# The first four blocks of the input projection computed together, chunk by chunk, with six blocks held in PSUM until the row scale is there

## The chip, the cores and the metric

The kernel runs on one NeuronCore of one Trainium2 chip. The metric is device microseconds of one launch. Engines are named as in the profile: PE is the matmul engine (TensorE), DVE is VectorE, ACT is ScalarE, POOL is GpSimd, and SP issues the transfers. Each engine works through its own instructions in a fixed order; semaphores make one engine wait for another.

## The reference

Two transformer-like blocks stand one behind the other, on one sequence of 512 rows of 1024 features, in float32. The change sits in the input projection of the first block. Cut to that, the reference is:

```python
def rms_norm(x, g):
    y = x * lax.rsqrt(jnp.mean(x * x, axis=-1, keepdims=True) + 1e-5)
    return y * g

def first_block(x, ...):                      # x: 1 x 512 x 1024
    xn = rms_norm(x, mix_norm)
    proj = xn @ w_in + b_in                   # 1024 -> 4352
    q, k, v, cb, cc, cx, ga, gc = split(proj) # 512, 128, 128, 3 x 512, 2 x 1024
    attn = sliding_window_attention(q, k, v, sinks)   # 8 heads, 2 KV heads, window 128
    conv = cb * causal_depthwise_conv(cc * cx, conv_w)
    merged = sigmoid(ga) * (attn @ w_attn_branch) + sigmoid(gc) * (conv @ w_conv_branch)
    h = x + merged @ w_out
    up = causal_depthwise_conv(rms_norm(h, ffn_norm) @ w_up, ffn_conv_w)
    gate, val = split(up)
    h = h + (silu(gate) * val) @ w_down       # 2816 hidden
    return rms_norm(h, final_norm)
```

The second block projects again, mixes with a sparse attention, a stick-breaking attention and a gated recurrence, projects out and ends in a layer norm. The change does not touch it.

## The kernel before

**Layout and products.** Activations lie transposed: a tile is 128 features by 512 rows of the sequence, and the model's 1024 features are eight such chunks (`KT = 8`). A weight block is 128 output features by all 1024 inputs (512 KB). To keep float32 accuracy each operand is split into a high and a low part: ACT writes the high part (`A.copy`, or `A.activation` with the norm's weight as scale), DVE subtracts it from the original for the low part (`split_w` for weights, `split` for x). One chunk of one block is then three PE products of 128x512: high weights by high x, high weights by low x, low weights by high x. A block is 24 products into one PSUM bank; the input projection has 34 blocks.

**The row scale.** The projection is done on x times the norm's weight, not yet divided by each row's root mean square. That row scale (`rstd1`, a 128x512 tile) comes from squares that ACT and DVE add up into one tile, one matmul with ones (`rms_scale`, bank `gb`) and a chain: a `tensor_scalar` on DVE, Ln and Exp on ACT, and four DVE steps (one Newton step). Each finished block is multiplied by it as it leaves its bank (`scaled`), and only then is the bank free. Before, blocks 0 and 1 are computed, the row sum's matmul is called for behind block 1 (`pre` at `n == 1`), and the block loop goes on.

**Banks and buffers.** The eight banks are pools: `m` 2, `ga` 2, `gb` 2, `oa` 1, `ob` 1. Blocks 0 to 3 take `m`, `oa`, `m`, `ob` (`alt`), later ones take `m`. Attention uses `ga` and `gb` for scores and transposes and `oa`, `ob` for its output. Raw weights (`raw`), high parts (`wh`) and low parts (`wl`) have two buffers each.

**The order of the work.** All weights and x come through SP's queue, in the program's order. `drive` interleaves the projection and the attention as generators, by the costs that they yield: attention advances at a quarter of the projection's rate, once blocks 0 to 5 (four of queries, one of keys, one of values) are done. A scheduler then fixes each engine's order. At the start block 0's weights come in three pieces between the chunks of x, and ten small matmuls on a tile of ones (`WARM`) occupy PE until the first data are there.

The rest of the kernel has the same pattern: weight blocks streamed through two buffers, products on PE, and elementwise work between.

Of the kernel before, what the change touches and what calls it, by code (L numbers as in the profile page):

```python
# [18 lines left out]
P = 128  # L19
T = 512  # L20
D = 1024
KT = 8
# [31 lines left out]
        IN2[(_n, _i) if _c else _n] = len(IN2)  # L54


WARM = 10
RATE_A = [0.593, 0.587, 0.591, 0.741, 0.778]
RATE_B = [0.318, 0.367, 0.286, 0.332, 0.497]
ORDER = [('gf', 0), ('gq', 0), 'kc', ('gi', 0), 'ng', 'vc', ('nq', 0), ('gf', 1), ('gq', 1), ('nq', 2), 'kw', 'ks', 'vs', ('bq', 0), ('gi', 1), ('gf', 2), 'vw', ('bk', 0), ('nq', 1), ('bv', 0), ('gq', 2), ('gi', 2), ('bq', 1), ('bk', 1), ('bv', 1)]  # L60
# [6 lines left out]
def tile_net(ctx, tc, a, out):  # L67
    nc = tc.nc
# [112 lines left out]
    def raw_tile():  # L181
        return wp.tile([P, 8, P], F32, tag="raw", name=nm("raw"), bufs=2)
# [6 lines left out]
    def split_w(raw, cuts=(0, 8)):  # L189
        nk, w = raw.shape[1], raw.shape[2]  # L190
        wh = wp.tile([P, 8, P], F32R, tag="wh", name=nm("wh"), bufs=2)[:, :nk, :w]
        wl = wp.tile([P, 8, P], F32R, tag="wl", name=nm("wl"), bufs=2)[:, :nk, :w]
        with tc.high_priority(offset=100):
            for c0, c1 in zip(cuts, cuts[1:]):
                c = slice(c0, min(c1, nk))
                A.copy(wh[:, c], raw[:, c])  # L196
                tt(wl[:, c], raw[:, c], wh[:, c].bitcast(F32), ALU.subtract)
        return wh, wl
# [45 lines left out]
    def alt(n):  # L244
        return ("m", "oa", "m", "ob")[n % 4]

    def split(src, scale=None, new=None):
        h, l = new(F32R), new(F32R)
        if scale is None:
            A.copy(h, src)  # L250
            tt(l, src, h.bitcast(F32), ALU.subtract)
        else:
            A.activation(h, src, AF.Copy, scale=scale)
            stt(l, src, scale, h.bitcast(F32), ALU.mult, ALU.subtract)
        return h, l
# [19 lines left out]
    def rms_scale(sq, dst):  # L275

        ps = bank("gb")
        for n, s in enumerate(sq):
            mm(ps, ones, s, n == 0, n == len(sq) - 1)
        ms = wk()  # L280
        V.tensor_scalar(ms, ps, 1.0 / D, 1e-5, ALU.mult, ALU.add)
        rsqrt(ms, dst)
# [14 lines left out]
        return cp.tile([P, T], F32, tag="rs", name=n, bufs=1)  # L297


    smt = cp.tile([P, SMW], F32, tag="smt", name="smt")  # L300
    nc.sync.dma_start(smt, a["small"])
    W1 = Weights([(a["w_in"][n], 8) for n in range(34)])
    raw = raw_tile()
    W1.raw.append(raw)
    xin = []
    cuts = (0, 2, 4, 8)
    for k in range(KT):
        t = tl("np")
        nc.sync.dma_start(t, a["xT"][k])
        xin.append(t)  # L310
        if k < 3:
            c = slice(cuts[k], cuts[k + 1])
            nc.sync.dma_start(raw[:, c], a["w_in"][0, :, c])
        elif k == 5:
            W1.ahead(2, 0)
    W1.ahead(3, 0)
    cst = cp.tile([P, CMW], F32, tag="cst", name="cst")
    nc.sync.dma_start(cst, a["const"])

    def S(n, i=0, w=None):  # L320
        o, full = SM[n]
        return smt[:, o + i:o + i + (full if w is None else w)]
# [19 lines left out]
        mm(warm[:, 0:P], ones, ones)  # L342


    W1.w.append(split_w(raw, cuts))
    xs = [split(xin[k], S("mix", k, 1), xt) for k in range(KT)]
    sq = []
    with tc.issue_after(last_act()):
        for k in range(KT):
# [12 lines left out]
    rstd1 = rs_tile("rs1")  # L362
# [86 lines left out]
        return use  # L449

    def in_proj():
        hold = []
        for n in range(34):
            yield from dense(W1, xs, use_in(n), (lambda: rms_scale(sq[:1], rstd1)) if n == 1 else None,
                             alt(n) if n < 4 else "m", hold=hold if n < 2 else None)

    def softmax_a(j, ip):

# [151 lines left out]
    for i in range(2):  # L610
        oh = wk()
        nc.sync.dma_start(oh[0:33], a["onehot"][:, 512 * i:512 * i + 512])
        ps = bank("ga")
# [635 lines left out]
    for half in range(2):  # L1249
        ps = [bank(t) for t in (("ga", "ga", "oa", "ob"), ("m", "m", "gb", "gb"))[half]]  # L1250
# [96 lines left out]
def _blocks(w):  # L1347
    k, n = w.shape
    return w.reshape(k // P, P, n // P, P).transpose(2, 1, 0, 3)


def _layout(i):
    pair = lambda step: np.concatenate([np.r_[64 * j:64 * j + 64, 64 * (j + step):64 * (j + step) + 64] for j in range(step)])
    q1 = pair(4)
    cin = [q1, 512 + np.arange(256)]
    for j in range(4):
        for base in (1280, 1792, 768):
            cin.append(base + P * j + np.arange(P))
    for j in range(8):
        for base in (2304, 3328):  # L1360
            cin.append(base + P * j + np.arange(P))
    cin = np.concatenate(cin)
    q2 = pair(3)
    off = np.cumsum([0, 384, 128, 128, 128, 128, 128, 128, 18, 384, 256, 256, 256, 256, 384, 384, 384, 384])
    nq, kc, vc, ks, vs, kw, vw, ng, nz, bq, bk, bv, bz, gq, gf, gi, gz = off[:-1]
    r = np.arange
    cin2 = np.concatenate([
        nq + q2, kc + r(128), vc + r(128), ks + r(128), vs + r(128), kw + r(128), vw + r(128),
        bq + r(256), bk + r(256), bv + r(256), gq + r(384), gf + r(384), gi + r(384),
        nz + q2, bz + r(256), gz + r(384),  # L1370
    ])
    rmix = np.concatenate([q2, r(384, 1024)])
    f = np.float32
    w_in, w_in2 = i["w_in"][0], i["w_in_2"][0]
    const, cmi, oh = _constants()
    pos = i["cmp_pos_2"][0].reshape(16, 2, 64).transpose(2, 1, 0).reshape(64, 32)
    small = {
        "mix": _cols(i["mix_norm"][0]), "ffn": _cols(i["ffn_norm"][0]), "fin": _cols(i["final_norm"]),
        "bin": _cols(i["b_in"][0][cin]),
        "cw": i["conv_w"][0].reshape(3, 4, P).transpose(2, 1, 0).reshape(P, 12),  # L1380
        "fcw": i["ffn_conv_w"][0].reshape(3, 44, P).transpose(2, 1, 0).reshape(P, 132),
        "sink": np.broadcast_to(i["sinks"][0], (P, 8)),
        "pos": np.concatenate([pos, pos], axis=0),
        "hgn": _cols(i["hg_norm_w_2"][0]), "lb": _cols(i["hg_lb_2"][0]),
    }
    up = _blocks(i["w_up"][0])
    br = np.concatenate([_blocks(i["w_attn_branch"][0][q1]), _blocks(i["w_conv_branch"][0])], axis=2)
    wo2 = i["w_out_2"][0][rmix]
    return {
        "xT": i["x"][0].T.reshape(KT, P, T),  # L1390
        "small": np.concatenate([small[n] for n in SM], axis=1),
        "const": const, "cmask": cmi, "onehot": oh,
        "tbl": np.concatenate([i["rel_bias_2"], np.full((1, 6), NEG, f)], axis=0),
        "w_in": _blocks(w_in[:, cin]),
        "w_br": br,
        "w_out": _blocks(i["w_out"][0]),
        "w_up": np.stack([up[:NFF], up[NFF:]], axis=1).reshape(2 * NFF, P, KT, P),
        "w_down": _blocks(i["w_down"][0]),
        "w_in_2": _blocks(w_in2[:, cin2]),
        "w_gate": w_in2[:, ng:ng + 18].reshape(KT, P, 18).transpose(1, 0, 2),  # L1400
        "w_ck1": i["w_ck1_2"][0].reshape(16, P, P).transpose(1, 0, 2), "w_ck2": i["w_ck2_2"][0],
        "w_cv1": i["w_cv1_2"][0].reshape(16, P, P).transpose(1, 0, 2), "w_cv2": i["w_cv2_2"][0],
        "w_out_2": wo2.reshape(KT, P, 2, T).transpose(2, 0, 1, 3),
        "ln_g": i["ln_g_2"], "ln_b": i["ln_b_2"],
    }
# [17 lines left out]
```

## Time and profile before

| | |
|---|---|
| median of 3 runs | 1068.86 us (1068.28 to 1069.32) |
| the profiled execution | 1068.53 us |
| its span, first to last instruction | 1066.8 us |
| PE busy | 1039.5 us, 97% of the span |
| DVE, ACT, POOL busy | 704.4 us (66%), 488.8 us (46%), 44.0 us (4%) |
| DMA | 97.84 MB, mean 92 GB/s |
| mean granted TensorE clock | 0.999 of 2.4 GHz |

The span is the time from the first to the last instruction of the profiled execution; 1.7 us of its own time lie around it. Busy shares are averages over the whole kernel. A matmul's duration in the trace includes the pipeline's tail, so two that follow each other overlap; the pace is read from start to start.

### The profile page before, as it was taken

What the parts mean: (1) busy time and instruction counts of PE and PEld (TensorE: products, weight loads), DVE (VectorE), ACT (ScalarE), POOL (GpSimd) and SP (SyncE); (2) the same over time, 40 slices, a digit from 0 to 9 for tenths busy, and PEclk for the clock granted to TensorE, in tenths of its full rate; (3) what the DMA queues carried; (4) which work ended last, traced back from release to release, by engine and by line L of the source; (5) the groups of instructions that cost most, each with busy time, mean ns of one, the idle gap of its engine ahead of it and who ended that gap; (6) DMA issues with size and microseconds to landing.
All of it is one profiled execution on the core that took longest, in us unless ns stands there. A gap on an engine that the chain in (4) does not pass through costs nothing.

```text
span 1066.8 us, 14636 instructions
## 1 busy us (share of the span) xinstructions
PE 1039.5 (97%) x5712; PEld 838.9 (79%) x5712; DVE 704.4 (66%) x1313; ACT 488.8 (46%) x855; POOL 44.0 (4%) x89
## 2 busy tenths in 40 slices
PE   8999999999999999999999999999999999989997
PEld 6788888888888888888877888767777777767886
DVE  6876643356448777777763233597967698887757
ACT  5754443322344444444442222433625676578740
POOL 0000000000220000000000111200000000011000
PEclk9999999999999999999999999999999999999999
DMA  6212232333432233223335333531321110101232
GB/s 218 79 60 80 79 94 85 99 99 109 142 120 85 98 99 99 98 99 99 99 94 193 97 106 90 184 101 41 99 75 47 59 41 22 41 21 37 82 120 79
DMA packets 32801, 97.84 MB, mean 92 GB/s; under 512 B 4878, under 2 KB 5390, under 8 KB 32732
## 3 DMA queue, kind: packets, MB, share of 16 engines
q1 hardware_dynamic: 32732, 96.91, 28.7%
q8 instruction: 45, 0.74, 0.3%
q14 instruction: 24, 0.20, 0.1%
HBM read 94.77 MB, written 5.27 MB: 94 GB/s over the span
## 4 chain that ended last, share of the span: by engine, by line
PE 75%; DVE 11%; ACT 7%; DMA 3%; issue 2%; SPq 1%; POOL 1%; DVEq 0%; POOLq 0%; ACTq 0%
PE pm L139 44%; PE pob L139 12%; PE poa L139 12%; PE pga L139 4%; PE pgb L139 3%; DVE wl L136 2%; DMA raw<-in_w_in 1%; ACT wh L196 1%; DVE lv L136 1%; DMA raw<-in_w_down 1%; DVE hk L136 1%; DVE dk L136 1%; DVE np L136 1%; DVE nk L942 1%; ACT nk L948 1%
## 5 line engine op out<-in xcount | busy, mean ns | idle before, releaser
L139 PE MATMUL pm<-x,wh 128*128 128x512 f32 (+1 forms) x1360 | 433.4, 395 | 2.1 <-DVE x L133 0.9
L139 PEld LDWEIGHTS pm<-x,wh 128*128 128x128 f32 (+1 forms) x1360 | 252.2, 187 | 58.5 <-issue 3.5
L196 ACT CAST wh<-raw 128x1024 fp32r<-128x1024 f32 (+1 forms) x153 | 156.7, 1025 | 275.8 <-issue 109.9
L139 PE MATMUL pm<-x,wl 128*128 128x512 f32 (+1 forms) x680 | 268.3, 395 | 0.0
L136 DVE TENSOR_TENSOR wl<-raw,wh 128x1024 fp32r<-128x1024 f32 (+1 forms) x153 | 181.9, 1189 | 89.5 <-ACT wh L196 87.7
L139 PEld LDWEIGHTS pm<-x,wl 128*128 128x128 f32 (+1 forms) x680 | 127.0, 187 | 26.8 <-issue 1.6
L139 PE MATMUL poa<-x,wh 128*128 128x512 f32 x208 | 65.0, 394 | 0.0
L139 PE MATMUL pob<-x,wh 128*128 128x512 f32 x208 | 64.1, 390 | 0.0
L139 PE MATMUL pm<-np,wh 128*128 128x512 f32 x176 | 54.1, 389 | 0.0
L136 DVE TENSOR_TENSOR dk<-pm,rs 128x512 f32<-128x512 f32 x43 | 29.5, 686 | 28.1 <-PE pm L139 28.0
L139 PEld LDWEIGHTS poa<-x,wh 128*128 128x128 f32 x208 | 39.0, 188 | 9.3 <-issue 1.0
L139 PEld LDWEIGHTS pob<-x,wh 128*128 128x128 f32 x208 | 39.0, 188 | 8.0
L136 DVE TENSOR_TENSOR nk<-pm,rs 128x512 f32<-128x512 f32 x34 | 23.4, 687 | 32.6 <-PE pm L139 32.4
L139 PE MATMUL poa<-x,wl 128*128 128x512 f32 x104 | 40.6, 390 | 0.1
L139 PE MATMUL pob<-x,wl 128*128 128x512 f32 x104 | 40.6, 390 | 0.0
L139 PEld LDWEIGHTS pm<-np,wh 128*128 128x128 f32 x176 | 33.0, 188 | 6.8
L139 PE MATMUL pm<-np,wl 128*128 128x512 f32 x88 | 34.2, 389 | 0.0
L948 ACT ACTIVATE nk<-nk,q 128x128 f32<-128x128 f32 (+3 forms) x48 | 26.5, 555 | 11.5 <-DVE q L946 11.2
L942 DVE CUSTOM_DVE_ANT_0 nk<-pgb,bi 128x128 f32<-128x128 f32 (+3 forms) x48 | 23.1, 484 | 7.9 <-PE pgb L139 7.2
L133 DVE SCALAR_TENSOR_TENSOR dk<-nk,smt,dk 128x511 f32<-128x511 f32 (+1 forms) x34 | 25.4, 748 | 1.4 <-ACT dk L435 0.8
L139 PE MATMUL pgb<-np,np 128*128 128x128 f32 (+3 forms) x96 | 25.9, 351 | 0.4 <-DVE nk L967 0.3
L133 DVE SCALAR_TENSOR_TENSOR nk<-nk,smt,nk 128x511 f32<-128x511 f32 (+2 forms) x33 | 24.7, 747 | 0.5
(498 smaller groups left out, 1664.7 us busy)
## 6 DMA issues: line engine op xcount, KB each, us to landing
raw<-in_w_in SPq DMA_DIRECT2D x65, 512.0 KB, 3.5
raw<-in_w_up SPq DMA_DIRECT2D x44, 512.0 KB, 3.5
raw<-in_w_down SPq DMA_DIRECT2D x16, 512.0 KB, 3.6
raw<-in_w_br SPq DMA_DIRECT2D x8, 512.0 KB, 3.4
raw<-in_w_out SPq DMA_DIRECT2D x8, 512.0 KB, 3.5
raw<-in_w_out SPq DMA_DIRECT2D x16, 256.0 KB, 2.7
raw<-in_w_down SPq DMA_DIRECT2D x8, 384.0 KB, 3.2
d<-d SPq DMA_DIRECT2D x6, 512.0 KB, 6.6
```

The source lines that it names most:

```text
L133: V.scalar_tensor_tensor(o, i0, s, i1, op0, op1)
L136: V.tensor_tensor(o, i0, i1, op)
L139: return TE.matmul(o, l, r, start=start, stop=stop)
L196: A.copy(wh[:, c], raw[:, c])
L942: V.tensor_tensor_reduce(pb[:, 0:Wd_], s[:, 0:Wd_], bias[h][:, T - Wd_:T], 1.0, -3e38, ALU.add, ALU.max, st[:, g:g + 1])
L948: A.activation(pbs[g][:, 0:Wd_], pbs[g][:, 0:Wd_], AF.Exp, bias=st[:, 2 + g:3 + g], accum_out=st[:, 4 + g:5 + g])
```

## The change

The first four blocks (the queries) are no longer computed one behind the other. A second copy of their weights, `w_in_4`, is laid out by chunk: for each of the eight chunks 128 x 4 x 128 elements (256 KB), fetched right behind that chunk of x. PE takes each chunk for all four blocks, twelve products at a time, into four banks. Block 4 (keys) and block 5 (values) then go one behind the other into the two `ga` banks. The row sum's matmul is called for behind block 5 in place of block 1, and the results of all six blocks are held in their banks until the row scale is there. The constants are fetched before block 4's weights, the small table of biases and norms behind the first chunk of x, and eight small matmuls are made at the start in place of ten.

```diff
-WARM = 10
+WARM = 8
...
     smt = cp.tile([P, SMW], F32, tag="smt", name="smt")
-    nc.sync.dma_start(smt, a["small"])
-    W1 = Weights([(a["w_in"][n], 8) for n in range(34)])
-    raw = raw_tile()
-    W1.raw.append(raw)
-    xin = []
-    cuts = (0, 2, 4, 8)
+    W1 = Weights([(a["w_in"][n], 8) for n in range(4, 34)])
+    xin, raws = [], []
     for k in range(KT):
         t = tl("np")
         nc.sync.dma_start(t, a["xT"][k])
+        if k == 0:
+            nc.sync.dma_start(smt, a["small"])
+        if k % 2 == 0:
+            raws.append(raw_tile())
+        nc.sync.dma_start(raws[-1][:, 4 * (k % 2):4 * (k % 2) + 4], a["w_in_4"][k])
         xin.append(t)
-        if k < 3:
-            c = slice(cuts[k], cuts[k + 1])
-            nc.sync.dma_start(raw[:, c], a["w_in"][0, :, c])
-        elif k == 5:
-            W1.ahead(2, 0)
-    W1.ahead(3, 0)
     cst = cp.tile([P, CMW], F32, tag="cst", name="cst")
     nc.sync.dma_start(cst, a["const"])
+    W1.ahead(1, 0)
...
-    W1.w.append(split_w(raw, cuts))
-    xs = [split(xin[k], S("mix", k, 1), xt) for k in range(KT)]
+    xs, w4 = [], []
+    for k in range(KT):
+        xs.append(split(xin[k], S("mix", k, 1), xt))
+        if k % 2 == 0:
+            w4.append(split_w(raws[k // 2], (0, 4, 8)))
...
     def in_proj():
-        hold = []
-        for n in range(34):
-            yield from dense(W1, xs, use_in(n), (lambda: rms_scale(sq[:1], rstd1)) if n == 1 else None,
-                             alt(n) if n < 4 else "m", hold=hold if n < 2 else None)
+        ps = [bank(alt(n)) for n in range(4)]
+        for k in range(KT):
+            (wh, wl), c = w4[k // 2], 4 * (k % 2)
+            xh, xl = xs[k]
+            for n in range(4):
+                mm(ps[n], wh[:, c + n], xh, k == 0, False)
+            for n in range(4):
+                mm(ps[n], wh[:, c + n], xl, False, False)
+                mm(ps[n], wl[:, c + n], xh, False, k == KT - 1)
+            yield 2.6
+
+        hold = [(use_in(n), ps[n]) for n in range(4)]
+        for n in range(4, 34):
+            yield from dense(W1, xs, use_in(n), (lambda: rms_scale(sq[:1], rstd1)) if n == 5 else None,
+                             "ga" if n < 6 else "m", hold=hold if n < 6 else None)
...
+        "w_in_4": w_in[:, cin[:512]].reshape(KT, P, 4, P),
```

How this moves instructions is seen at three places of the engines' orders. The numbers in names are those of the tiles; they differ between the two kernels.

First place, PE at the matmul of the row sums (`pgb` from a tile `nk` and `ones`). In the kernel before, it stands inside block 2 (`pm_282`), and block 3 (`pob_322`) follows:

```order
L139 MATMUL pm_282<-x_152,wh_223 128x512
L139 MATMUL pgb_251<-nk_160,ones 128x512
L139 MATMUL pm_282<-x_153,wh_223 128x512
L139 MATMUL pm_282<-x_152,wl_224 128x512
L139 MATMUL pm_282<-x_156,wh_223 128x512
L139 MATMUL pm_282<-x_157,wh_223 128x512
L139 MATMUL pm_282<-x_156,wl_224 128x512
L139 MATMUL pob_322<-x_128,wh_285 128x512
```

In the changed kernel it stands behind the last product of block 5 (`pga_348`), and block 6 (`pm_575`) follows, in the bank that block 0 (`pm_209`) has held:

```order
L139 MATMUL pga_348<-x_176,wh_320 128x512
L139 MATMUL pga_348<-x_177,wh_320 128x512
L139 MATMUL pga_348<-x_176,wl_321 128x512
L139 MATMUL pgb_379<-nk_180,ones 128x512
L139 MATMUL pm_575<-x_124,wh_351 128x512
L139 MATMUL pm_575<-x_125,wh_351 128x512
L139 MATMUL pm_575<-x_124,wl_352 128x512
```

Before, 29 products that need no scaled block stand between that matmul and block 4, the first to reuse a bank; now none does.

Second place, DVE around the chain of the row scale, from the last low parts of weights to the first scaled blocks. Before (`dk_264` is block 0 scaled):

```order
L281 TENSOR_SCALAR dk_253<-pgb_251 128x512
L136 TENSOR_TENSOR wl_326<-raw_221,wh_325 128x1024
L136 TENSOR_TENSOR nk_259<-nk_255 128x512
L136 TENSOR_TENSOR nk_259<-nk_259,dk_253 128x512
L272 TENSOR_SCALAR nk_259<-nk_259 128x512
L136 TENSOR_TENSOR rs_183<-nk_255,nk_259 128x512
L136 TENSOR_TENSOR dk_264<-pm_189,rs_183 128x512
```

In the changed kernel (`wl_579` belongs to block 7, `dk_392` is block 0 scaled):

```order
L136 TENSOR_TENSOR wl_352<-raw_312,wh_351 128x1024
L136 TENSOR_TENSOR wl_579<-raw_314,wh_578 128x1024
L281 TENSOR_SCALAR dk_381<-pgb_379 128x512
L136 TENSOR_TENSOR nk_387<-nk_383 128x512
L136 TENSOR_TENSOR nk_387<-nk_387,dk_381 128x512
L272 TENSOR_SCALAR nk_387<-nk_387 128x512
L136 TENSOR_TENSOR rs_203<-nk_383,nk_387 128x512
L136 TENSOR_TENSOR dk_392<-pm_209,rs_203 128x512
```

The low part of block 7 now stands ahead of the chain; on ACT the cast of the same block (`wh_578`, into the buffer of block 5) stands ahead of the chain's Ln as well.

Third place, PE where attention begins (`pga`, `pgb` from `hk`, keys, and `gp`, queries, are scores; `pga` from `cst` and `nk` are the transposes of the values). Before, this is at the first product of block 6 (`pm_571`):

```order
L139 MATMUL pm_571<-x_128,wh_411 128x512
L139 MATMUL pgb_449<-hk_397,gp_268 128x128
L139 MATMUL pgb_479<-hk_397,gp_268 128x256
L139 MATMUL pm_571<-x_129,wh_411 128x512
L139 MATMUL pm_571<-x_128,wl_412 128x512
```

In the changed kernel it is behind the fourth product of block 7 (`pm_616`):

```order
L139 MATMUL pm_616<-x_134,wh_578 128x512
L377 MATMUL pga_446<-cst,nk_443 128x128 x4
L139 MATMUL pm_616<-x_135,wh_578 128x512
L139 MATMUL pm_616<-x_134,wl_579 128x512
L139 MATMUL pga_452<-hk_431,gp_395 128x128
L139 MATMUL pm_616<-x_138,wh_578 128x512
L139 MATMUL pm_616<-x_139,wh_578 128x512
L139 MATMUL pm_616<-x_138,wl_579 128x512
L139 MATMUL pga_452<-hk_433,gp_395 128x128
```

The scores of attention's first unit have moved back by one block and five products. From the last third of block 11 on, PE's order is the same in both kernels, and so are the other engines' from about there.

## Rows read from the trace of the kernel before

**Rows 1.** The page, its list of busy time, share of the span and instructions of each engine.

```profile
PE 1039.5 (97%) x5712; PEld 838.9 (79%) x5712; DVE 704.4 (66%) x1313; ACT 488.8 (46%) x855; POOL 44.0 (4%) x89
```

**Rows 2.** What PE waited for between 80 and 250 us (total, times, longest), and one stretch of 20 us from the table of stretches (stretch, length, then busy us and instructions of PE, PEld, DVE, ACT, POOL, then granted clock, DMA share, GB/s).

```profile
PE pob L139 <- ACT dk L435: 0.3, 1, 0.3
...
100.00:120.00 20.00, 19.98 (x104) 16.40 (x103) 13.36 (x29) 9.40 (x24) 0.00 (x0) 1.00 0.25 79
```

**Rows 3.** The timeline of PE over the first 26 us (start us, us, engine line operation out<-in xcount; in brackets the idle time before it and what ended it; a row that merges several instructions has their count behind x).

```profile
1.13 4.64 PE L139 MATMUL pgb<-ones 128*128 128x128 f32 x20 [1.13 <-POOL ones L338]
...
5.42 0.89 PE L139 MATMUL pm<-x,wh 128*128 128x512 f32 x2
...
24.10 0.62 PE L139 MATMUL pm<-x,wh 128*128 128x512 f32 x2
...
24.78 0.39 PE L139 MATMUL pm<-x,wh 128*128 128x512 f32 x1
...
25.10 1.12 PE L139 MATMUL pgb<-nk,ones 128*128 128x512 f32 x2
```

**Rows 4.** The start: ACT at its first activations of x and its third cast of block 0 (timeline), and what the DMA engines moved in the first 30 us, in 40 slices of 0.75 us.

```profile
4.09 0.72 ACT L253 ACTIVATE x<-np,smt 128x512 fp32r<-128x512 f32 x1 [1.69 <-DMA np<-in_xT]
...
8.77 0.62 ACT L196 CAST wh<-raw 128x512 fp32r<-128x512 f32 x1 [0.21 <-DMA raw<-in_w_in]
...
GB/s 0 0 73 255 300 371 146 247 298 339 317 295 309 385 407 404 426 378 370 211 107 224 390 81 0 0 0 87 279 328 5 0 109 360 229 22 0 0 0 0
```

**Rows 5.** The timeline from the matmul of the row sums to the first product of block 4, on DVE, ACT and PE.

```profile
26.26 0.69 DVE L281 TENSOR_SCALAR dk<-pgb 128x512 f32<-128x512 f32 x1 [1.22 <-PE pgb L139]
...
26.98 0.63 ACT L267 ACTIVATE nk<-dk 128x512 f32<-128x512 f32 x1 [5.25 <-DVE dk L281]
...
28.46 0.63 ACT L268 ACTIVATE nk<-nk 128x512 f32<-128x512 f32 x1
...
28.59 1.23 DVE L136 TENSOR_TENSOR wl<-raw,wh 128x1024 fp32r<-128x1024 f32 x1 [1.64 <-ACT wh L196]
...
29.73 0.69 DVE L136 TENSOR_TENSOR nk<-nk 128x512 f32<-128x512 f32 x1
...
30.45 0.69 DVE L136 TENSOR_TENSOR nk<-nk,dk 128x512 f32<-128x512 f32 x1
...
31.18 0.43 DVE L272 TENSOR_SCALAR nk<-nk 128x512 f32<-128x512 f32 x1
...
31.64 0.69 DVE L136 TENSOR_TENSOR rs<-nk,nk 128x512 f32<-128x512 f32 x1
...
32.37 0.69 DVE L136 TENSOR_TENSOR dk<-pm,rs 128x512 f32<-128x512 f32 x1
...
32.66 1.05 ACT L196 CAST wh<-raw 128x1024 fp32r<-128x1024 f32 x1 [3.57 <-PE pob L139]
...
33.20 0.70 PE L139 MATMUL pm<-x,wh 128*128 128x512 f32 x2 [0.36 <-DVE dk L136]
```

**Rows 6.** The first and the seventh of ACT's steps that make queries, keys and values out of scaled blocks (with no cast of weights between these two), and DVE's four subtractions for the keys.

```profile
33.61 0.72 ACT L414 ACTIVATE dk<-dk,b 128x512 f32<-128x512 f32 x1
...
37.41 0.72 ACT L414 ACTIVATE nk<-nk,b 128x512 f32<-128x512 f32 x1
...
43.76 2.79 DVE L136 TENSOR_TENSOR hk<-nk,hk 64x512 fp32r<-64x512 f32 x4
```

**Rows 7.** PE at the first product of block 6, at the first score, at the first product behind the first unit's scores, and at the first product of block 8 (timeline).

```profile
44.20 0.39 PE L139 MATMUL pm<-x,wh 128*128 128x512 f32 x1
...
45.51 0.50 PE L139 MATMUL pgb<-hk,gp 128*128 128x128 f32 x2 [0.92 <-ACT hk L395]
...
49.98 0.40 PE L139 MATMUL pm<-x,wh 128*128 128x512 f32 x1
...
65.08 0.62 PE L139 MATMUL pm<-x,wh 128*128 128x512 f32 x2
```

**Rows 8.** The first unit's softmax: ACT's first exponential, DVE's mask on one tile of scores (with its maximum), ACT's last pair of exponentials, DVE's sum, the first scaling of the probabilities, their transposes on PE, ACT's copy of some, and DVE's copy of the second half's.

```profile
50.79 0.40 ACT L480 ACTIVATE dk<-dk,q 128x128 f32<-128x128 f32 x1 [1.43 <-DVE q L476]
...
51.47 0.48 DVE L473 CUSTOM_DVE_ANT_0 dk<-pgb,cst,smt 128x256 f32<-128x256 f32 x1
...
52.57 0.47 ACT L482 ACTIVATE q<-q,smt 128x2 f32<-128x2 f32 x2
...
53.07 0.17 DVE L136 TENSOR_TENSOR q<-q 128x4 f32<-128x4 f32 x1 [0.90 <-ACT q L482]
...
53.48 0.55 DVE L490 TENSOR_SCALAR dk<-dk,q 128x128 f32<-128x128 f32 x2
...
54.12 0.49 PE L500 MATMUL pga<-cst,dk 128*128 128x128 f32 x3
...
56.23 0.46 ACT L503 COPY nk<-pgb 128x384 f32<-128x384 f32 x1
...
58.79 0.68 DVE L503 COPY nk<-pga 128x512 f32<-128x512 f32 x1
```

**Rows 9.** The table of stretches at the end of the kernel (columns as in rows 2; the granted clock is the third number from the right, 1.00 being 2.4 GHz and 0.50 1.2 GHz).

```profile
1059.00:1060.00 1.00, 0.23 (x2) 0.02 (x1) 0.70 (x2) 0.00 (x0) 0.00 (x0) 1.00 0.81 307
...
1063.00:1064.00 1.00, 0.00 (x0) 0.00 (x0) 0.77 (x2) 0.00 (x0) 0.00 (x0) 0.97 0.04 14
...
1064.00:1065.00 1.00, 0.00 (x0) 0.00 (x0) 0.00 (x0) 0.00 (x0) 0.00 (x0) 0.50 0.99 377
```


## The prediction

> **What bounds the kernel now.** I read the busy times first: PE is busy for 97% of the span, DVE for 66%, ACT for 46% [rows 1]. That alone doesn't make PE the bound everywhere, so I looked at what PE waits for, by stretches. Between 80 and 250 us it waits 0.3 us in all, and a stretch of 20 us there is full [rows 2]: in the input projection, behind its first 65 us, time lost or won on PE is lost or won for the kernel. What is left open is the first 65 us, and there I went through PE's timeline from start to start. Three 128x512 products take 0.68 us (24.10 to 24.78), 0.2267 each, so a block takes 5.44 us [rows 3]. The first product starts at 5.42, and the 67th ends its turn at 25.0, where the matmul of the row sums follows [rows 3]; 67 products need 15.2 us, so PE stands as if it had begun at 9.8 without a gap. Some 4.4 us are lost while x arrives. Block 4 waits 0.36 us for the first scaled block [rows 5]. Block 6 begins at 44.20, block 8 at 65.08 [rows 7]; these two are my marks for comparison.
>
> **The start (a gain).** Before, one chunk of x feeds three products of one block, 0.7 us of PE; now it feeds twelve, 2.72 us. Chunk and weights are 524 kB. The DMA engines moved 1,043 kB in the first 6 us and about 220 kB or more per 0.75 us after that [rows 4], so a chunk takes about 1.8 us of transfer, under the 2.72 of PE: PE should be fed from the first chunk on. ACT and DVE have a split of x and half a weight tile per chunk, 0.72 + 0.62 us on ACT [rows 4], also under 2.72.
>
> When does it begin? The first chunk needs x, the table and its weights, 262 + 127 + 262 = 651 kB, which the same slices reach at 4.24. Before, x and table (389 kB, moved by 3.5) were usable at 4.09, 0.6 later; the third piece of block 0 (1,437 kB, moved by 7.1) at 8.77, 1.65 later [rows 4]. So the weights are usable between 4.85 and 5.9, the cast takes 0.62, and PE begins between 5.55 and 6.6. I take 5.8, nearer the first, since few transfers are in flight by then. Six blocks are 144 products, 32.64 us: block 5 ends at **T = 38.45**. Against the 9.8 of before this gains 4.0 us. Two edits cost nothing here: eight warm-up matmuls end, at 0.23 us for each half [rows 3], by 4.9, ahead of the data. The transfer for chunk 4 now waits in SP's queue for a raw buffer (the subtraction of chunk 1, about 9.3), with chunks 5 to 7 behind it; PE wants chunk 4 at 5.8 + 4 x 2.72 = 16.7, over 7 us later, against 1.8 of moving and at most 1.65 of lag. Without that cover it would cost what it is late.
>
> **The row scale (a loss).** The chain stands behind block 5, and block 6 needs block 0's bank; nothing stands between on PE. On ACT the cast of block 7's weights is ahead of Ln. It needs the buffer of block 5, so it can start only as block 5 ends, as the cast at 32.66 waited for block 3 [rows 5]. On DVE the subtraction of the same weights is ahead of the chain's first step. From T on, all by [rows 5]: cast 1.05 + 0.03; subtraction to next instruction 1.14 (28.59 to 29.73); first step to Ln 0.72; Ln and Exp 0.68 + 0.66; from the first DVE step behind Exp to PE's product 3.47 (29.73 to 33.20). That is 7.75 us: **R = 46.2** for the first product of block 6, with PE idle for some 6.5 of it. Before, that product stood at 44.20. So the first two terms together are **+2.0**: 4.0 gained, 6.0 lost. If the cast and the subtraction were out of the way, the matmul's 1.16 (25.10 to 26.26) would stand in place of 2.2, and R were 1.0 earlier.
>
> **Attention's first scores (a loss).** Behind the waiting product stand all of attention and the later blocks. Before, ACT and DVE made queries, keys and values while PE computed blocks 4 and 5. Now six results come free at once. ACT has 18 steps for them, one behind the other, at 0.633 us (six from 33.61 to 37.41, [rows 6]), from R - 0.1 on. PE reaches the transposes of the values after 28 products, at R + 6.35; they need ACT's 14th step, R + 8.8. The transposes and two products more, then the first score needs the 16th, R + 10.05; three products, then the third score needs the 18th, R + 11.3; the last keys' subtractions on DVE (0.70 each, [rows 6]) end at R + 12.2. The last scores need eight small matmuls behind that: PE gets to its next product at R + 13.3, with 33 products done. Before, seven products and the same unit took 44.20 to 49.98 [rows 7], including a wait of 0.92, so with 26 products more it would be 11.7. The difference is **+1.6**.
>
> **The first softmax (a loss).** Fifteen products follow, to R + 16.7; the unit's rest follows without any product between, where before 17 products stood ahead of it and more within it. On DVE four masks (0.4 each) end at R + 13.8, then the subtraction of block 8's weights stands ahead of the next step: R + 14.95. Exponentials take ACT 2.25 (50.79 to 53.04), sum to transposes 1.05 (53.07 to 54.12) [rows 8]: PE waits until R + 18.3, 1.6 us. ACT's copy of transposes comes behind four exponentials more, R + 20.4; PE is there at R + 20.0, 0.4. DVE's copy of the second half's transposes (0.68) comes behind four scalings, four masks and block 9's subtraction, R + 24.85; PE is there at R + 23.4, 1.5. I take **+3.5** for the three; block 8 begins at R + 26.0 = 72.2, against 65.08. From there on products stand between attention's steps again, and I find no wait on the way to block 11, from where PE's order is as before.
>
> **The sum.** -4.0 + 6.0 + 1.6 + 3.5 = +7.1 us. The profiled execution took 1068.53, 0.3 under the median; I add to its time: **1075.6 us**. Bounds: the start -0.25 to +0.8, the chain -1.0 to +0.5, attention's two terms together between 0 (ACT and DVE never late) and 7.
>
> **The clock.** At the end of the kernel PE stops at about 1059.2 and the granted clock reads 1.00 until it falls in the slice from 1063 to 1064 to 0.50, the 1.2 GHz level [rows 9]: 4.7 us of idleness. The new wait of 6.5 us is longer, so block 6 may begin at 1.2 GHz. From the kernel's first matmul at 1.13 to its first product at 5.42 [rows 3] it had been kept busy 4.3 us; if as long is spent at half pace behind R, 2.1 us of work are lost. I count nothing: PE would reach the transposes at R + 8.45, still ahead of R + 8.8. Without that cover it would be +2.1.
>
> The Trainium skill (TensorE: Matmul & The Clock Gate, Part 1) says that an idle TensorE falls back to half its clock and gets it back only behind sustained activity; the trace agrees on the fall, and no row shows the return. By the rule the sum stays at 1075.6, and were the cover gone it would be 1077.7.
>
> **The rivals.**
>
> *Only the row-scale chain counts.* ACT and DVE are quicker behind R than I walk, since no other casts of weights stand among their 18 steps, and attention's waits are no longer than before. For it speaks that ACT is busy for 46% only; against it that steps on one engine stand one behind the other whatever the average. +2.0: 1070.5, between 1069.0 and 1072.
>
> *The clock rises late at the start.* Now PE pauses about a microsecond between warm-up and products. If this keeps the low level for as long as the first stretch, 4.3 us, twelve-product chunks run at half pace and 2.1 us are lost on top: 1077.7. Nothing before shows a pause there.
>
> *The start isn't bound by PE.* The chunks come no faster than x did, and the 4.0 us aren't won: 1079.6. Against it speaks the transfer rate above.
>
> *Faster.* One quantity decides: the sum of PE's waits between T and block 8. In my walk it is 6.5 for the chain and 6.7 for attention, 13.2 us. If DVE and ACT serve PE so quickly there that it falls below 13.2 - 9.2 = 4.0, the kernel is over 2.1 us faster, about 1066. Six dependent DVE steps and two on ACT in the chain alone take longer than that [rows 5], unless the trace's durations hide that steps can overlap.
>
> **How the numbers follow.** My forecast (+4 to +9) has 0.64; only the chain 0.18; clock 0.09; start 0.04; faster 0.05. What a measurement of this kernel can tell from no change is about 0.2%, 2.1 us. The second case straddles that, so half of it, 0.09, is within; faster 0.05; slower 0.86. The range from 1070.5 to 1079 leaves out the faster case, half of the second and part of the start's case, about 0.17.
>
> **What would show it.** In the changed profile: the first product between 5.5 and 6.6 and gaps under 0.3 us up to block 5's end near 38.5; one wait of PE on DVE's first scaled block of 6 to 7 us; the granted clock dipping to 0.50 around R; waits of PE on ACT (value bias, keys) of some 3 us in block 7, and on DVE in front of block 8; block 8 near 72. I am wrong if the wait on the scaled block is under 4 us, if attention's waits don't appear, or if time comes back behind block 11.

## The result and the profile after

The changed kernel takes 1078.59 us in the median of four executions (1076.58 to 1082.13), the kernel before beside it 1069.07: a ratio of 1.0087 (95% interval 1.0065 to 1.0109). Timed a second time it was 1078.70 against 1069.66, 1.0092 (1.0078 to 1.0105). It is slower, by 9 us in the median and by 8.1 us in the profiled execution, whose time is 1076.58 and whose span is 1074.9 (before 1068.53 and 1066.8). The forecast was 1075.6, from 1070.5 to 1079.0. The profiled execution is the fastest of the nine that were timed; four of the nine lie above 1079.0. Two single executions below, one of the early scale and one of the 13 warm-ups, were disturbed and are left out; they were the profiled ones, so these two kernels have times but no trace that is read here.

The page's busy times, to be read beside [rows 1], and what PE waited for in the first 90 us (total, times, longest):

```profile
PE 1039.9 (97%) x5708; PEld 841.0 (78%) x5708; DVE 704.3 (66%) x1315; ACT 488.9 (45%) x857; POOL 44.1 (4%) x89
...
PE pm L139 <- DVE dk L136: 6.7, 1, 6.7
PE pm L139 <- ACT wh L196: 2.0, 1, 2.0
PE pgb L139 <- POOL ones L335: 1.1, 1, 1.1
PE pga L511 <- DVE dk L501: 1.1, 1, 1.1
PE poa L139 <- DVE nk L514: 0.9, 1, 0.9
```

The busy times of PE, DVE and ACT have moved by 0.4 us at most; what is new is idle time. One row is 6.7 us: PE at block 6, waiting for DVE's first scaled block, where [rows 5] has 0.36.

The timeline of PE at the places that answer to [rows 3] and [rows 7]: the first product, the matmul of the row sums, block 6, the transposes of the values, the first product behind the first unit's scores, and block 8.

```profile
6.91 0.50 PE L139 MATMUL pm<-x,wh 128*128 128x512 f32 x1 [2.00 <-ACT wh L196]
...
39.69 1.02 PE L139 MATMUL pgb<-nk,ones 128*128 128x512 f32 x2
...
47.39 1.19 PE L139 MATMUL pm<-x,wh 128*128 128x512 f32 x2 [6.67 <-DVE dk L136]
...
56.66 0.60 PE L377 MATMUL pga<-cst,nk 128*128 128x128 f32 x4
...
60.64 0.63 PE L139 MATMUL pm<-x,wh 128*128 128x512 f32 x2
...
72.51 0.73 PE L139 MATMUL pm<-x,wh 128*128 128x512 f32 x2
```

From 6.91 to 39.69 PE has no gap: 144 products, 0.228 us each. The chain behind it on ACT and DVE, to be laid beside [rows 5]:

```profile
39.66 1.04 ACT L196 CAST wh<-raw 128x1024 fp32r<-128x1024 f32 x1 [3.08 <-PE pga L139]
40.73 1.22 DVE L136 TENSOR_TENSOR wl<-raw,wh 128x1024 fp32r<-128x1024 f32 x1 [4.21 <-PE pgb L139]
41.88 0.68 DVE L281 TENSOR_SCALAR dk<-pgb 128x512 f32<-128x512 f32 x1
42.59 0.63 ACT L267 ACTIVATE nk<-dk 128x512 f32<-128x512 f32 x1 [1.89 <-DVE dk L281]
...
46.55 0.69 DVE L136 TENSOR_TENSOR dk<-pm,rs 128x512 f32<-128x512 f32 x1
```

The order is the forecast one: cast and subtraction of block 7's weights first, then the chain, each step behind the one before. The cast waited for PE's last product of block 5 (its bracket), as the prediction had it from the one buffer.

The table of stretches around that wait (stretch, length, PE busy, granted clock, DMA share, GB/s):

```profile
42.00:43.00 1.00, 0.00 (x0) 1.00 0.05 16
43.00:44.00 1.00, 0.00 (x0) 0.56 0.83 233
44.00:45.00 1.00, 0.00 (x0) 0.50 0.68 274
...
51.00:52.00 1.00, 1.00 (x4) 0.50 0.00 0
...
53.00:54.00 1.00, 1.00 (x5) 0.82 0.00 0
```

PE has nothing to do from 40.7 to 47.4. The clock falls to its 1.2 GHz level in the slice from 43 to 44 and comes back in the slice from 53 to 54, some 6 us after PE began block 6; until then products start 0.43 us apart.

Behind block 8 the distance to the kernel before grows little: 7.43 us there, 7.57 at POOL's first addition near 280 us, 8.14 at the one near 590, 8.1 at the end.

### The profile page after: what moved, and what is told of

Read it like the earlier page. It is cut to its first block, busy times and chain, and to the rows that moved or that the text cites. A ratio compares the mean times of both kernels' runs of the same rounds, so it can differ in the third digit from the quotient of the medians.

```text
span 1074.9 us, 14632 instructions
## 1 busy us (share of the span) xinstructions
PE 1039.9 (97%) x5708; PEld 841.0 (78%) x5708; DVE 704.3 (66%) x1315; ACT 488.9 (45%) x857; POOL 44.1 (4%) x89
## 4 chain that ended last, share of the span: by engine, by line
PE 78%; DVE 11%; ACT 6%; DMA 2%; issue 2%; POOL 1%; SPq 0%; DVEq 0%; POOLq 0%; ACTq 0%
PE pm L139 45%; PE poa L139 12%; PE pob L139 12%; PE pga L139 5%; PE pgb L139 3%; DVE wl L136 2%; DVE hk L136 1%; DVE lv L136 1%; DMA raw<-in_w_down 1%; DVE nk L953 1%; ACT wh L196 1%; ACT nk L959 1%; DVE dk L136 1%; DVE np L136 1%; PE pgb L976 1%
## 5 line engine op out<-in xcount | busy, mean ns | idle before, releaser
L139 PE MATMUL pm<-x,wh 128*128 128x512 f32 x1328 | 426.4, 396 | 8.7 <-DVE dk L136 6.7
L139 PEld LDWEIGHTS pm<-x,wh 128*128 128x128 f32 x1328 | 247.1, 188 | 62.8 <-issue 10.3
L196 ACT CAST wh<-raw 128x1024 fp32r<-128x1024 f32 (+2 forms) x155 | 157.0, 1014 | 286.4 <-issue 113.9
L139 PE MATMUL pm<-x,wl 128*128 128x512 f32 x664 | 262.7, 396 | 0.0
L136 DVE TENSOR_TENSOR wl<-raw,wh 128x1024 fp32r<-128x1024 f32 (+2 forms) x155 | 182.5, 1178 | 101.4 <-ACT wh L196 95.6
L139 PEld LDWEIGHTS pm<-x,wl 128*128 128x128 f32 x664 | 124.7, 188 | 26.4 <-issue 1.1
```

What stands on the lines that cost most here:

```text
L136: V.tensor_tensor(o, i0, i1, op)
L139: return TE.matmul(o, l, r, start=start, stop=stop)
```

## The experiments

**The changed kernel again**, for its spread (no edit).

> The changed kernel once more, beside the kernel before and the experiments, for its own spread: its four times lay between 1076.6 and 1082.1 us, ten times the spread of the kernel before. Theory (the wait for the row scale and attention's late start make the loss, the clock's fall is mostly covered): median 1076 to 1079, and a mean granted clock that goes with the time. Rival (the clock is a term of its own): times of 1076 to 1082, longer where the mean granted clock is lower.

1078.70 us (1078.09 to 1081.64), profiled at 1078.23. The row-scale wait is 6.7 us again, but the start differs. PE at its first two products and at the first ones of full pace:

```profile
6.51 0.80 PE L139 MATMUL pm<-x,wh 128*128 128x512 f32 x1 [1.60 <-ACT wh L196]
7.11 0.63 PE L139 MATMUL poa<-x,wh 128*128 128x512 f32 x1
...
10.07 0.39 PE L139 MATMUL pm<-x,wh 128*128 128x512 f32 x1
10.31 0.40 PE L139 MATMUL pm<-x,wl 128*128 128x512 f32 x1
...
40.95 1.02 PE L139 MATMUL pgb<-nk,ones 128*128 128x512 f32 x2
```

PE begins 0.4 us earlier than in the other profile and finishes block 5 at 40.95, 1.26 later. The first eight products come 0.43 us apart, the later ones 0.23. This is the rival in which the clock rises late at the start; it happens in some executions of this kernel and not in others. Of the nine, the mean granted clock is lowest (0.989) in the two slowest, but it is 0.991 at 1078.09 us as well as at 1081.22, so it goes with the time only in part.

**The hold alone.** The kernel before, with the six blocks held and the row sum behind block 5; the start stays block by block.

```diff
-            yield from dense(W1, xs, use_in(n), (lambda: rms_scale(sq[:1], rstd1)) if n == 1 else None,
-                             alt(n) if n < 4 else "m", hold=hold if n < 2 else None)
+            yield from dense(W1, xs, use_in(n), (lambda: rms_scale(sq[:1], rstd1)) if n == 5 else None,
+                             alt(n) if n < 4 else "ga" if n < 6 else "m", hold=hold if n < 6 else None)
```

> The kernel before with the hold alone: block after block as before, but the row sum's matmul behind block 5 and six results held, blocks 4 and 5 in the ga banks. Theory: the start stays (block 5 ends near 42.5 us), block 6 waits 6.7 us and begins near 50.2, 6.0 later than before; attention costs 4.2 more, as in the changed kernel; 1078 to 1080 in all. Rival (the hold is cheap, and the chunks are what costs): 1070 or less.

1079.18 us (1078.39 to 1080.95), ratio 1.0091 (1.0077 to 1.0104). PE at the row sums and at block 6:

```profile
42.19 1.02 PE L139 MATMUL pgb<-nk,ones 128*128 128x512 f32 x2
...
49.90 1.19 PE L139 MATMUL pm<-x,wh 128*128 128x512 f32 x2 [6.68 <-DVE dk L136]
```

The distance from one to the other is 7.71 here and 7.70 in the changed kernel. So the hold, with the row sum behind block 5, makes the whole loss by itself, and the chunk-by-chunk start gives back less than was forecast: the traces near 280 us are 10.15 (hold alone), 8.90 and 7.57 (with chunks) behind the kernel before, 1.3 to 2.6 us in place of 4.0, and the medians do not tell the two apart.

**The scale early.** The changed kernel, with the row scale made as soon as the four chunked blocks are done; only these four are held, until then.

```diff
-        hold = [(use_in(n), ps[n]) for n in range(4)]
+        rms_scale(sq[:1], rstd1)
+        for n in range(4):
+            use_in(n)(ps[n])
...
-            yield from dense(W1, xs, use_in(n), (lambda: rms_scale(sq[:1], rstd1)) if n == 5 else None,
-                             "ga" if n < 6 else "m", hold=hold if n < 6 else None)
+            yield from dense(W1, xs, use_in(n), None, "ga" if n < 6 else "m")
```

> The changed kernel with the row sum's matmul right behind the eight chunks, ahead of block 4, and blocks 0 to 3 alone held until then; blocks 4 and 5 are scaled as they end. Theory (the wait for the row scale is the loss, the chunks are a gain): no wait of PE at block 6, which begins near 40.8 us (39.7 + 1.07) in place of 47.4; attention's scores in block 7 still wait 2 to 3 us for ACT, whose 18 steps start near 36.5, and the first softmax costs as in the changed kernel; 1067 to 1070 in all. Rival (the order by chunks itself, with four banks in turn, is what costs): still 1075 or more.

1068.82 us (1066.64 to 1072.87), ratio 0.9989 (0.9977 to 1.0001): 10 us under the changed kernel, with the same chunked start. The place of the row scale, and the hold that goes with it, carry the loss.

**PE kept busy during the wait.** 26 products into an unused bank behind the row sum's matmul; they add work that the reference doesn't have.

```diff
+        def scale_and_fill():
+            rms_scale(sq[:1], rstd1)
+            fill = bank("gb")
+            for _ in range(26):
+                mm(fill, xs[0][0][:, 0:P], xs[0][0])
...
-            yield from dense(W1, xs, use_in(n), (lambda: rms_scale(sq[:1], rstd1)) if n == 5 else None,
+            yield from dense(W1, xs, use_in(n), scale_and_fill if n == 5 else None,
```

> The changed kernel with 26 products more on PE between the row sum's matmul and block 6, into a bank that nobody reads (5.9 us, so they end 0.7 us before the first scaled block is there). PE's clock has then no reason to fall. Theory (the clock's fall is covered by ACT's steps): block 6 begins when it did, 7.7 us behind block 5's end; the transposes of the values wait for ACT until 8.8 us behind block 6's start where they came at 9.3; at most 0.5 us is won in the profiled execution, 1076 in all. Rival (the clock is a term of its own): the 5 us at half pace and the spread go, 1074 or less, with all times within 1.5 us.

1084.51 us (1083.71 to 1085.66), ratio 1.0136. PE at the filler, at block 6, at the transposes of the values, and further on:

```profile
41.43 6.47 PE L139 MATMUL pgb<-x 128*128 128x512 f32 x26
48.69 0.70 PE L139 MATMUL pm<-x,wh 128*128 128x512 f32 x2 [0.79 <-DVE dk L136]
...
57.57 0.66 PE L377 MATMUL pga<-cst,nk 128*128 128x128 f32 x4 [0.44 <-ACT nk L422]
...
67.42 0.70 PE L517 MATMUL pga<-cst,dk 128*128 128x128 f32 x3 [3.78 <-DVE dk L507]
```

Block 6 starts no earlier and runs at full clock; in return PE now waits for ACT at the transposes, 8.88 us behind block 6's start. That is the cover that the prediction named. The total misses the expectation: attention is ordered differently in this kernel (its one more bank in use is the likely reason, not a shown one), with a new wait of 3.78 us, and 4.85 us more were lost near 585 us, at a wait of 3.2 us (0.7 before) with products at half pace behind it. As a test of the total this kernel says nothing.

**The small table first**, ahead of the first chunk of x (one execution).

```diff
+        if k == 0:
+            nc.sync.dma_start(smt, a["small"])
         nc.sync.dma_start(t, a["xT"][k])
-        if k == 0:
-            nc.sync.dma_start(smt, a["small"])
```

> The changed kernel with the small table fetched ahead of the first chunk of x again, as before. Theory (the first weights of the chunks are late, 5.8 to 6.2 us, since 650 kB stand ahead of PE's first product, whatever their order): the first cast between 5.8 and 6.3, PE's first product between 6.5 and 6.9. Rival (the table's place costs it): the first cast 0.4 us earlier or more.

1078.85 us. The first weights are cast at 5.11, earlier than the expected 5.8 to 6.3, and PE begins at 5.78; but its first eleven products come at the low pace, until 10.6, and block 5 ends at 40.88. Against the second profile above, 0.7 us is won at the first product and no more than 0.1 is left of it at block 5's end. Nor is the 0.7 shown to be the table's doing: with the table behind x, the same cast begins anywhere from 4.67 to 6.41 in the seven other traces of kernels with chunks.

**Thirteen warm-up matmuls**, first in the changed kernel, then in the one with the early scale.

```diff
-WARM = 8
+WARM = 13
```

> The changed kernel with 13 warm-up matmuls in place of 8, nothing else; at the first ones' pace they end near 6.7 us, about when the first weights are there, and PE has no pause ahead of its first product. Theory (the spread of the changed kernel, 1076 to 1082 us, is the clock at the start: in one profiled execution the first products went at 0.227 us, in another the first eight at 0.427, and block 5 ended at 39.7 and 41.0): the first products at 0.227 in every execution, times within 2 us of each other, median 1076 to 1077. Rival (the spread comes from the clock's fall behind block 5, or from elsewhere): median and spread as before, 1078.7 and 4 us.

1078.09 us (1074.98 to 1079.54), ratio 1.0069 (1.0049 to 1.0088), against 1.0087 and 1.0092: not told apart. The times spread over 4.6 us, as the rival had it, and not within 2. One more execution, for its trace:

> The changed kernel with 13 warm-up matmuls once more, for its trace. If the warm-ups decide the pace of the first products, they come at 0.227 us each from the first on, and block 5 ends 32.6 us behind the first product (39.0 to 39.8); the row-scale wait is 6.7 us as before. If the level at the start comes by chance, the first products may come at 0.427 here as well, and block 5 ends near 41.

1078.69 us. PE's first product starts at 6.17 at full pace, block 5 ends at 38.95, and block 6 begins at 46.65 behind the same wait of 6.68; near 280 us the kernel is 6.86 behind. It then loses 2.2 us near 580, a place that the section on the hardware shows.

> The row sum's matmul ahead of block 4 (as in e1) and 13 warm-up matmuls. Theory: block 6 begins near 40.8 us with no wait for the row scale, the granted clock stays at 1.00 from the first product on; attention waits 4 to 6 us in blocks 7 and 8; 1066 to 1068, within 2 us of each other. Rival (the order by chunks costs by itself): no faster than the kernel before, block 6 behind 43 us.

1068.33 us (1067.24 to 1072.75), ratio 0.9989 (0.9977 to 1.0001): full pace from the first product, and no gain over the early scale alone that the medians show; the spread is 5.5 us and not 2. PE at blocks 6 and 8:

```profile
40.12 0.62 PE L139 MATMUL pm<-x,wh 128*128 128x512 f32 x2
...
63.53 0.73 PE L139 MATMUL pm<-x,wh 128*128 128x512 f32 x2
```

Block 6 begins 4.1 us ahead of the kernel before (44.20), block 8 only 1.55 (65.08). In between PE waits 2.9 us for attention's steps (1.08, 0.20, 0.79, 0.87), against 1.1 in the kernel before. So in this trace attention takes back 2.5 of the 4.1 us, most of it in waits, though nothing waits for the row scale.

**Attention two blocks later.** One line, in three kernels: the one with early scale and 13 warm-ups, the kernel before, and the changed kernel.

```diff
-        yield from need(*[("in", n) for n in range(6)])
+        yield from need(*[("in", n) for n in range(8)])
```

> As e6, and attention is let in only once blocks 6 and 7 are done as well, so that the first scores stand behind block 7 and block 8 is between them and the softmax's transposes. Theory (what remains of the loss is attention's ScalarE and VectorE steps, which stand too close to the products that feed them): PE's waits between block 6 and block 12 fall under 1.5 us, another 3 to 5 us are won over e6, 1063 to 1065. Rival (attention's waits only move, or its end comes too late for what needs it): as e6 or slower.

1065.27 us (1064.70 to 1066.47), ratio 0.9956 (0.9941 to 0.9972): faster than both kernels, just above the expected 1063 to 1065. What PE waits for between 0 and 110 us, beyond the start (for ACT's first weights and POOL's ones), is two rows:

```profile
PE pga L512 <- DVE nk L502: 0.3, 1, 0.3
PE pob L139 <- ACT dk L435: 0.2, 1, 0.2
```

> The kernel before with one line changed: attention begins behind blocks 0 to 7 in place of blocks 0 to 5. If the gain of the best version so far (early row scale, 13 warm-ups, attention two blocks later: 4.1 us under the kernel before) comes from attention's start alone, this kernel gains as much, about 1065 us. If it needs the chunk-by-chunk start too, it gains only the waits that the first scores and the first softmax have in the kernel before (0.9 us at the first score, and some tenths on the way to block 11), about 1067.5 to 1069. In the trace the first marks stay: block 4 at 33.2, no wait of PE on keys.

1070.00 us (1067.76 to 1073.68), ratio 1.0011 (0.9999 to 1.0023). That is above the expected 1067.5 to 1069: the later attention alone gains nothing. The 4.1 us need the chunked start too, and by the next kernel the early scale; whether they need the 13 warm-ups was not tried.

> The changed kernel with the same one line: attention behind blocks 0 to 7. The hold and the wait of 6.7 us stay as they are. If the loss behind that wait comes from attention standing too close behind the six results that come free at once (1.6 + 2.65 us in the profile of the changed kernel), it goes: about 1074 to 1075, and block 6 still begins 7.7 us behind block 5. If the loss there has another cause (the low clock behind the wait, 26 columns' worth of products at half pace), it stays: 1078 to 1079. If the low clock was hidden by the wait on ACT, it now comes out: some 2 us of the 4 stay, 1076.

1073.69 us (1072.30 to 1075.36), ratio 1.0042 (1.0028 to 1.0057): half of the loss is gone though the hold stands, a little more than expected. PE at the row sums, in block 6 and at the transposes of the values:

```profile
39.34 1.02 PE L139 MATMUL pgb<-nk,ones 128*128 128x512 f32 x2
47.04 1.19 PE L139 MATMUL pm<-x,wh 128*128 128x512 f32 x2 [6.68 <-DVE dk L136]
48.03 0.63 PE L139 MATMUL pm<-x,wl 128*128 128x512 f32 x1
...
53.10 0.39 PE L139 MATMUL pm<-x,wl 128*128 128x512 f32 x1
...
58.36 0.66 PE L377 MATMUL pga<-cst,nk 128*128 128x128 f32 x4
```

The row-scale wait is untouched; the waits of attention are gone, bar 0.5 us in all. Now the low clock shows: 14 products take from 47.04 to 53.10, 6.06 us where 14 x 0.2267 = 3.17 would do, 2.9 us lost. At the mark near 280 us the kernel is 4.50 behind, against 7.57 in the changed one. Of the 4.50, 2.84 stand at block 6 already (47.04 against 44.20), so 1.66 are left behind it, less than the clock's 2.9, because the kernel before has waits there of its own that the later attention does away with (0.92 in [rows 7]).

## Why the prediction held, and by how much its terms missed

The sign, the mechanism and the range held: one long wait, attention late behind it, and no time given back behind block 11. The median lies only 0.4 us inside the range. Against the trace of the profiled execution the sum of 7.1 us is measured as 8.1, and its terms are off in both directions; against the medians, 9.5 and 9.0 us, the sum is short by about 2. T is the end of block 5, R the start of block 6.

**The start (mis-sized).** Forecast: first product at 5.8, T = 38.45, 4.0 gained. Measured: 6.91 and 39.69, that is 2.8 gained. PE was fed without a gap, as forecast. The step that failed is the moment of the first weights, which rested on the transfer rate of the kernel before. ACT waited until 6.24 for them:

```profile
4.07 0.72 ACT L253 ACTIVATE x<-np,smt 128x512 fp32r<-128x512 f32 x1 [1.67 <-DMA smt<-in_small]
6.24 0.62 ACT L196 CAST wh<-raw 128x512 fp32r<-128x512 f32 x1 [1.45 <-DMA raw<-in_w_in]
```

What the DMA engines moved in half microseconds (columns as in the table of stretches above):

```profile
3.50:4.00 0.50, 0.50 (x4) 1.00 0.69 198
4.00:4.50 0.50, 0.50 (x5) 1.00 0.50 160
4.50:5.00 0.50, 0.41 (x2) 1.00 0.58 86
5.00:5.50 0.50, 0.00 (x0) 1.00 0.69 229
```

From 3.5 to 5.5 it is 86 to 229 GB/s; in the kernel before it was 314 and 385 in the first two of these slices and fell only then. The 651 kB that the first product needs were moved by 5.1 and not by 4.24, and the cast followed 1.1 later. What makes the rate dip there was not settled. The moment differs between executions: with this order of transfers the cast begins at 6.24 here, at 5.84 in the second profile, and at 4.67 to 6.41 in the five other traces, and in all seven some half microsecond between 4 and 5 has 205 GB/s or less. A first product at 5.8 wants the cast at 5.2, earlier than in six of the seven; this profile is one of the two latest. One reading of the rows was off as well: the 1,437 kB were moved by 7.25, not 7.1 [rows 4], so the latest moment for the weights would have been 5.76 and not 5.9; the measured one lies behind both.

**The clock at the start (a rival that occurs).** It was priced at 2.1 us, with a chance of 0.09. It came in the second profile of this kernel (1.26 us later at T, although 0.4 earlier at the first product), with the filler and with the small table first, and not in the first profile. The price was about right, as 1.7 us from first product to T (34.44 against 32.78); the mistake was to treat it as all or nothing, where executions differ. The median lies 2 us above the profiled execution; this, and the place near 580 us told of below, are what the traces show of that, though not every execution was traced; and with 13 warm-ups, where no trace has the low pace at the start, median and spread stayed as they were.

**The row scale (right).** R - T forecast 7.75, measured 7.70 in both profiles. Since T came 1.2 later, R came 1.2 later: +3.2 in place of +2.0.

**Attention's first scores (the time right, a sign of it missing).** The next product behind them was forecast at R + 13.3 and stands at R + 13.25; ACT's 14th step ends at R + 8.8, as forecast. But the waits of PE on ACT of some 3 us in block 7, named as a sign, are not in this profile. PE came to the transposes later than walked, at half pace, and the only wait for ACT is 0.33 us, at the third score (PEld is PE's weight load):

```profile
55.49 0.71 ACT L422 ACTIVATE nk<-nk,smt 128x512 f32<-128x512 f32 x1
...
58.68 0.19 PEld L139 LDWEIGHTS pgb<-hk,gp 128*128 128x128 f32 x1 [0.33 <-ACT hk L395]
```

That score starts at R + 11.3, the end of ACT's 18th step, as forecast. So ACT's steps set the time, and the slow clock filled the wait.

**The first softmax (somewhat too dear).** Three waits of 1.6, 0.4 and 1.5 us were forecast; the rows above have 1.1 and 0.9, and the middle one isn't there. Block 8 came at R + 25.12, not 26.0: +2.65 in place of +3.5, of which 2.0 are the two waits; for the other 0.7 the profile names no wait. DVE was a little quicker than walked, step by step: its four masks ended at R + 13.6 (forecast 13.8), and its copy of the second half's transposes at R + 24.05 (forecast 24.85).

**The clock behind the wait (hidden as forecast, by a later step than forecast).** It fell, and the transposes start at R + 9.27: PE reached them 0.46 behind ACT's step, not 0.35 ahead of it as forecast (R + 8.45), and it was the third score that took up the delay. How long the low level lasts differs between executions: 6.1 us here, 6.0 in the second profile, 3.4 with the small table first and with 13 warm-ups. The last of these, at block 6, at the first product of full pace, and at block 8:

```profile
46.65 1.19 PE L139 MATMUL pm<-x,wh 128*128 128x512 f32 x2 [6.68 <-DVE dk L136]
...
50.10 0.40 PE L139 MATMUL pm<-x,wl 128*128 128x512 f32 x1
...
71.79 0.73 PE L139 MATMUL pm<-x,wh 128*128 128x512 f32 x2
```

Block 8 stands at R + 25.1 in all four, so the fall costs nothing there, whether it lasts 3.4 or 6.1 us. Uncovered it would cost 1.6 us at 3.4 (8 products in 3.45 us in place of 1.81) and 2.9 at 6.1, as the changed kernel with the later attention shows; the forecast 2.1, from 4.3, lies between. The rule of the Trainium skill (TensorE: Matmul & The Clock Gate, Part 1) that full clock returns only behind sustained activity had no row before; these rows agree with it.

**Behind block 8.** 0.7 us more came later, of which 0.55 at a wait near 580 us, 1.25 against 0.70 us.

In sum 3.2 + 1.6 + 2.65 + 0.7 = 8.1. The experiments settle the cause: without the late row scale the loss is gone (1068.8), with it alone it is all there (1079.2), and moving attention out of the crowd behind R takes back 5 us of it (1073.7). The intervals of the three ratios do not overlap; the single terms are read from one trace each.

## What to carry to other kernels

A value that frees several banks should be made as early as its inputs allow: held results turn a chain of small steps on the other engines into idle time of the matmul engine, and everything that was spread between the blocks before then comes due at once behind it. A stall of several microseconds also leaves the clock low for the work behind it, which shows only when nothing else is waited for there. Order and timing of a consumer, here attention, is worth trying again after each change of its producers: the one line that gained nothing in the kernel before gained 3 us in the kernel with the chunked start and the early scale, and 5 us in the changed one.

## What the runs showed of the hardware

**The clock at the start differs between executions.** With 8 warm-up matmuls the first products came at 0.23 us each in two traces (the changed kernel, and it with the later attention) and at 0.43 for 8 to 11 products in three (it again, with the filler, with the small table first). The idle time between warm-up and first product does not sort them: 2.00 and 1.65 us in the first two, 1.60, 1.58 and 0.87 in the others. With 13 warm-ups all three traces had full pace. What decides it stays open. The granted clock reads 1.00 in these stretches whichever the pace, so the level was read from the starts of products.

**A short wait may bring the low clock, or not.** Near 573 us every kernel here waits for the down projection's weights, on ACT's cast and then on DVE's subtraction. In the kernel before with the later attention (timeline of PE, then stretches):

```profile
573.11 0.73 PE L139 MATMUL poa<-np,wh 128*128 128x512 f32 x2 [1.17 <-ACT wh L196]
574.37 0.50 PE L139 MATMUL poa<-np,wl 128*128 128x512 f32 x1 [0.53 <-DVE wl L136]
...
575.00:576.00 1.00, 1.00 (x4) 0.50 0.65 111
...
579.00:580.00 1.00, 1.00 (x6) 1.00 0.05 20
```

Waits of 1.17 and 0.53 us were followed by products at half pace for 3.4 us. The same happened in the best kernel (1.04 and 0.53; of 4.36 us ahead near 280 us it kept 2.41) and in the changed one with 13 warm-ups (1.31 and 0.52); behind 1.25 and 0.53 us in the changed kernel, 1.05 and 0.53 in the one with attention later, and 1.04 and 0.53 in the one with early scale and 13 warm-ups the clock stayed at 1.00. The length of the wait does not sort these six. A full fall and return costs about 2 us there, as much as the smaller differences measured here. It is also why a gain near the start need not arrive whole at the end.
